# One-hot rows of the expert gates made by whole-tensor operations with two tokens interleaved, and an index look-up summed by halves

## The chip, the cores and the metric

The kernel runs on one core of one Trainium2 chip. The core has five engines that run side by side, each through its own list of instructions in order: TensorE (PE in the profile, with PEld for its weight loads), VectorE (DVE), ScalarE (ACT), GpSimd (POOL) and SyncE (SP, which here only starts transfers). They wait for each other through semaphores. The metric is the device time of one execution, in microseconds (us).

## The reference

The program is two transformer blocks on 256 tokens of width 1024. The change lies in the last stage of the second block, a mixture of 16384 tiny experts. Cut to what matters:

```python
PEER_HEADS, PEER_NKEYS, PEER_TOPK = 8, 128, 16        # experts = 128 x 128

q = (xb @ w_q).reshape(tb, PEER_HEADS, 2, PEER_DKEY // 2)
s = jnp.einsum('thpd,hpnd->thpn', q, sub_keys)
sv, si = lax.top_k(s, k)                               # 16 best row keys, 16 best column keys
cand = sv[:, :, 0, :, None] + sv[:, :, 1, None, :]
cand_idx = si[:, :, 0, :, None] * PEER_NKEYS + si[:, :, 1, None, :]
top_v, top_i = lax.top_k(cand, k)                      # 16 of the 256 pairs
experts = jnp.take_along_axis(cand_idx, top_i, axis=-1)
g = jax.nn.softmax(top_v, axis=-1)
a = gelu(einsum('td,thkd->thk', xb, u[experts]))
return einsum('thk,thkd->td', g * a, v[experts])
```

## The kernel before

**No gather.** The kernel computes the activations of all 16384 experts for all tokens and multiplies them with a matrix that is the gate where a token chose the expert and zero elsewhere. The stage has two long passes. `u_pass` (4 calls, 64 pairs of row keys j) makes `gelu(u h2)`: for each j, 8 blocks of 128x128 weights, and for each block three matmuls of 256 tokens (lines 171 to 173), since every fp32 weight is split into a high half `whi` (ACT, line 133) and a low half `wlo` (DVE, line 130). So one j is 24 matmuls, one `whi` and one `wlo`. `v_pass` (4 calls) multiplies the activations with the gates and then with `v` (line 1095). Both weights stream from HBM through `raw` (line 154, issued by SP), 1 MB for a pair of j.

**The gate matrix.** It is built beside `u_pass` by a generator that `feed` steps once or twice after each pair. First `topk_steps`, for 128 tokens at a time (`tt`): top 16 by DVE, softmax `e_`, and for each of the 128 choices of a token (8 heads x 16) the row and the column key. These are looked up by comparing a position with 0..15 (`eq`, lines 960 and 965: 16 planes of 128 choices, all but one plane zero) and by summing the 16 planes (`ix`, line 970). Gates and keys are then transposed by PE so that a partition is a choice and a column a token: `idxT` (row key), `jdxT` (column key), `gT` (the gate in two fp16 parts).

Then `g_steps`, 32 groups of TG = 8 tokens. For each token the gate matrix is a product of two one-hot matrices over its 128 choices. DVE makes the one-hot rows `o1` for a group with one whole-tensor compare (line 1001), four tokens interleaved: the fastest index of `o1` runs over 4 tokens. It makes the gated one-hot rows `og` with one small instruction for each token and each of the two gate parts (line 1005), 16 for a group, each a compare with a per-partition key and a product with a per-partition gate:

```python
nc.vector.tensor_scalar(og[:, t, c], iota16, jdxT[:, tc_:tc_ + 1], gT[:, c, tc_:tc_ + 1],
                        op0=OP.is_equal, op1=OP.mult)
```

PE multiplies them a step later, 16 matmuls of 128 columns for a group (line 1016), ACT copies the result to `gs` (line 1018) and ACT's queue stores it to the HBM tensor `gg_d` (line 1019, `ggd` in the trace). `v_pass` reads it back as `gh` (line 1075), 8 transfers of 2 MB, issued by SP.

**What sets the order.** A scheduler arranges each engine's instructions from a simulated timeline, with program order as its priority. `o1` and `og` have three buffers, `gs` two, `whi` and `wlo` three each, `raw` three. DVE runs its list in order, so a `wlo` that stands behind a group's one-hot work waits for it, and PE's third matmul of a block waits for that `wlo`.

Of the kernel before, what the change touches and what calls it, by code (L numbers as in the profile page):

```python
# [10 lines left out]
F32 = mybir.dt.float32  # L11
F32R = mybir.dt.float32r
BF16 = mybir.dt.bfloat16
F16 = mybir.dt.float16
I32 = mybir.dt.int32
U32 = mybir.dt.uint32
AF = mybir.ActivationFunctionType
# [3 lines left out]
P = 128  # L21
# [42 lines left out]
def block_kernel(ctx: ExitStack, tc: tile.TileContext, a: dict, out: bass.AP, dbg=None):  # L64
# [796 lines left out]
    ga_d = [dram.tile([P, QJ // 2, 2 * S], F32, name=f"gad{q}") for q in range(2)]  # L861
    gg_d = dram.tile([P, NG, NE * TG], F32, name="ggd")

    idxT = big.tile([P, S], F16, name="idxT")
    jdxT = big.tile([P, S], F32, name="jdxT")
    gT = big.tile([P, 2, S], F32, name="gT")
    iota16 = big.tile([P, P], F16, name="iota16")
    nc.vector.tensor_copy(iota16, iota)
    iota4 = big.tile([P, P, 4], F16, name="iota4")
    nc.vector.tensor_copy(iota4, iota[:, :, None].to_broadcast([P, P, 4]))  # L870
    st4 = ExitStack()
    tk = pool(st4, "tk")
    keys = tk.tile([P, 16, P], F32, name="keys")
# [33 lines left out]
    def topk_steps():  # L907
        for tt in range(2):
            tv = tk.tile([P, 8, 16], F32, tag="tv", bufs=2, name="tv")
            ti = tk.tile([P, 8, 16], U32, tag="ti", bufs=2, name="ti")  # L910
            si = tk.tile([P, 8, 2, 16], U32, tag="si", bufs=2, name="si")
            for h in range(8):
                sv = tk.tile([P, 2, 16], F32, tag="sv", bufs=2, name="sv")
                for p_ in range(2):
                    s2 = tk.tile([P, P], F32, tag="s2", bufs=2, name="s2")
                    top16(sv[:, p_], si[:, h, p_], scs[h][:, 2 * tt + p_], s2)
                yield
                cd = tk.tile([P, NROW, 8], F32, tag="cd", bufs=2, name="cd")
                cd2 = tk.tile([P, NROW * 8], F32, tag="cd2", bufs=2, name="cd2")
                cf = cd.rearrange("p r c -> p (r c)")  # L920
                nc.vector.tensor_scalar(cf[:, 0:16], sv[:, 1], sv[:, 0, 0:1], None, op0=OP.add)
                nc.vector.tensor_tensor(cd[:, 2:9], sv[:, 0, 1:8, None].to_broadcast([P, 7, 8]),
                                        sv[:, 1, None, 0:8].to_broadcast([P, 7, 8]), op=OP.add)
                nc.vector.tensor_scalar(cd[:, 9], sv[:, 0, 8:16], sv[:, 1, 0:1], None, op0=OP.add)
                top16(tv[:, h], ti[:, h], cf, cd2)
                yield

            e_ = tk.tile([P, 8, 16], F32, tag="te", name="te")
            nc.vector.tensor_tensor(e_, tv, tv[:, :, 0:1].to_broadcast([P, 8, 16]), op=OP.subtract)
            nc.scalar.activation(e_, e_, AF.Exp)  # L930

            rc = tk.tile([P, 2, 8, 16], U32, tag="rc", name="rc")
            nc.vector.tensor_scalar(rc[:, 0], ti, 3, None, op0=OP.logical_shift_right)
            nc.vector.tensor_scalar(rc[:, 1], ti, 7, None, op0=OP.bitwise_and)
            rf = tk.tile([P, 2, 8, 16], F32, tag="rf", name="rf")
            nc.vector.tensor_copy(rf, rc)
            sf_ = tk.tile([P, 8, 2, 16], F16, tag="sf", name="sf")
            nc.vector.tensor_copy(sf_, si)
            yield
            z = small.tile([P, 8], F32, tag="az", name="tz")  # L940
            nc.vector.reduce_sum(z, e_, axis=AX.X)
            rz = small.tile([P, 8], F32, tag="ar", name="trz")
            nc.vector.reciprocal(rz, z)
            nc.vector.tensor_scalar(rz, rz, GSCALE, None, op0=OP.mult)
            nc.vector.tensor_tensor(e_, e_, rz[:, :, None].to_broadcast([P, 8, 16]), op=OP.mult)

            ij = tk.tile([P, 2, P], F16, tag="ij", name="ij")
            r_, c_ = (rf[:, x].rearrange("p h k -> p (h k)") for x in range(2))
            t_ = tk.tile([P, 3, P], F32, tag="ijt", name="ijt")
            nc.vector.scalar_tensor_tensor(t_[:, 0], r_, 9.0, c_, op0=OP.is_equal, op1=OP.mult)  # L950
            nc.vector.tensor_scalar(t_[:, 1], r_, -1.0, 0.0, op0=OP.add, op1=OP.max)
            nc.vector.tensor_tensor(ij[:, 0], t_[:, 0], t_[:, 1], op=OP.add)
            nc.vector.tensor_tensor(t_[:, 1], c_, t_[:, 0], op=OP.subtract)
            nc.vector.tensor_scalar(t_[:, 2], r_, 1.0, 8.0, op0=OP.is_equal, op1=OP.mult)
            nc.vector.tensor_tensor(ij[:, 1], t_[:, 1], t_[:, 2], op=OP.add)
            yield
            back = [(e_, None)]
            for p_ in range(2):
                eq = tk.tile([P, 16, P], F16, tag="eq", name="eq")
                nc.vector.tensor_tensor(  # L960
                    eq.rearrange("p j (g f) -> p j g f", f=4), iota4[:, :16, None, :].to_broadcast([P, 16, P // 4, 4]),
                    ij[:, p_].rearrange("p (g f) -> p g f", f=4)[:, None].to_broadcast([P, 16, P // 4, 4]),
                    op=OP.is_equal)
                eh = eq.rearrange("p j (h k) -> p j h k", h=8)
                nc.vector.tensor_tensor(
                    eh, eh, sf_[:, :, p_].rearrange("p h j -> p j h")[:, :, :, None].to_broadcast([P, 16, 8, 16]),
                    op=OP.mult)
                yield
                ix = tk.tile([P, P], F32, tag="ix", bufs=2, name="ix")
                nc.vector.reduce_sum(ix, eq.rearrange("p j x -> p x j"), axis=AX.X)  # L970
                back.append((ix, p_))
                yield
            with tc.issue_after(last_mm[0].ins):
                for src, p_ in back:
                    pt = ps_d()
                    ts = slice(tt * P, (tt + 1) * P)
                    nc.tensor.transpose(pt[:, :P], src if p_ is not None else src.rearrange("p h k -> p (h k)"), ident)
                    if p_ is None:
                        gt16 = tk.tile([P, P], F16, tag="gt16", name="gt16")
                        nc.scalar.activation(gt16, pt[:, :P], AF.Copy)  # L980
                        nc.scalar.activation(gT[:, 0, ts], gt16, AF.Copy)
                        nc.vector.tensor_tensor(gT[:, 1, ts], pt[:, :P], gT[:, 0, ts], op=OP.subtract)
                    else:
                        nc.scalar.activation((idxT, jdxT)[p_][:, ts], pt[:, :P], AF.Copy)

    def g_steps():

        gp = pool(stg, "gp", 3)
        todo = None
        for i in range(NG + 1):  # L990
            new = None
            if i < NG:
                ts = slice(i * TG, (i + 1) * TG)

                def four(x):
                    return x.rearrange("p (g t) -> p g t", t=4)[:, :, None, :].to_broadcast([P, TG // 4, P, 4])

                io = iota4[:, None].to_broadcast([P, TG // 4, P, 4])
                o1 = gp.tile([P, TG // 4, P, 4], F16, tag="o1", name="o1")
                og = gp.tile([P, TG, 2, P], F16, tag="og", name="og")  # L1000
                nc.vector.tensor_tensor(o1, io, four(idxT[:, ts]), op=OP.is_equal)  # L1001
                for t in range(TG):
                    for c in range(2):
                        tc_ = i * TG + t
                        nc.vector.tensor_scalar(og[:, t, c], iota16, jdxT[:, tc_:tc_ + 1], gT[:, c, tc_:tc_ + 1],  # L1005
                                                op0=OP.is_equal, op1=OP.mult)
                new = i, o1, og
            if todo:
                i_, o1, og = todo
                gs = gp.tile([P, NE, TG], F32, tag="gs", bufs=2, name="gs")  # L1010
                with tc.issue_after(last_mm[0].ins):
                    for g4 in range(TG // 4):
                        ps = (ps_d, ps_b)[g4 % 2]()
                        for t4 in range(4):
                            for c in (1, 0):
                                nc.tensor.matmul(ps[:, t4 * P:(t4 + 1) * P], o1[:, g4, :, t4], og[:, g4 * 4 + t4, c],
                                                 start=(c == 1), stop=(c == 0))
                        nc.scalar.activation(gs[:, :, g4 * 4:g4 * 4 + 4], ps.rearrange("p (t j) -> p j t", t=4), AF.Copy)
                nc.scalar.dma_start(gg_d[:, i_], gs.rearrange("p j t -> p (j t)"))
            todo = new  # L1020
            yield
# [253 lines left out]
```

## Time and profile before

| | us |
|---|---|
| median of 3 runs (lowest to highest) | 1461.04 (1459.24 to 1467.02) |
| the profiled execution | 1463.96 |
| its span, first to last instruction | 1462.0 |
| PE / DVE / ACT busy | 1388.6 / 1076.4 / 705.0 |

The span is what the trace covers; about 2 us of the execution lie around it. Busy shares are averages over the whole program, so the reading goes stage by stage: the look-ups run from about 640 to 745 us, the 32 groups from 822 to 1000 us, the rest of `u_pass` ends near 1100 us, and `v_pass` fills what follows up to 1448 us. In the rows PE's matmul durations contain waiting in the pipeline; the distance from one start to the next is what a matmul costs PE. The same holds on DVE: the chain of waits gives the time that one instruction adds to the chain, which is shorter than its duration.

### The profile page before, as it was taken

The numbers are of one execution on the slowest core, as the hardware profiler recorded it, in microseconds if no ns is written. First come the engines' busy times: TensorE is split into PE (matmuls) and PEld (weight loads), VectorE is DVE, ScalarE is ACT, GpSimd is POOL, SyncE is SP. The second block draws the span as 40 slices with busy tenths as digits, with TensorE's granted clock in tenths as the row PEclk, the third lists the DMA queues.
The fourth block names the chain that finished last, engine by engine and source line by source line (L and its number), as shares of the span: only waits on it lengthen the run. The fifth ranks groups of instructions, "written<-read, shape, count | busy, mean of one in ns | idle before, by whom it ended". The sixth has DMA issues, their size and how long they took to land.

```text
span 1462.0 us, 24629 instructions
## 1 busy us (share of the span) xinstructions
PE 1388.6 (95%) x9776; PEld 1278.8 (87%) x9776; DVE 1076.4 (74%) x2154; ACT 705.0 (48%) x1032; POOL 23.7 (2%) x25
## 2 busy tenths in 40 slices
PE   7999999999999999999999888889799999999997
PEld 6967998999998889999999888889788888888886
DVE  6774779998977556899964799995835555566765
ACT  4444645454545555554544434444334455444443
POOL 1000000000000010000000000000000000000000
PEclk9999999999999999999999989999989999999999
DMA  7442447777886414344555456668986555588762
GB/s 244 160 168 87 151 167 281 266 264 277 297 288 216 160 49 173 130 160 168 180 187 187 166 202 241 243 245 273 350 300 229 185 203 187 196 277 295 266 247 86
DMA packets 88451, 308.88 MB, mean 211 GB/s; under 512 B 6416, under 2 KB 39824, under 8 KB 61200
## 3 DMA queue, kind: packets, MB, share of 16 engines
q1 hardware_dynamic: 78544, 279.26, 54.8%
q10 hardware_dynamic: 9792, 28.05, 5.1%
q8 instruction: 76, 1.25, 0.4%
q14 instruction: 39, 0.32, 0.1%
HBM read 281.08 MB, written 26.21 MB: 210 GB/s over the span
## 4 chain that ended last, share of the span: by engine, by line
PE 75%; DVE 17%; DMA 5%; issue 2%; ACT 0%; POOL 0%; SPq 0%; POOLq 0%; DVEq 0%; ACTq 0%
PE acc L1095 24%; PE psa L173 9%; PE psa L171 9%; PE psa L172 9%; DVE og L1005 7%; PE psc L173 5%; PE psc L171 5%; PE psc L172 5%; DVE wlo L130 4%; DMA gh<-ggd 2%; DMA raw<-in_uT 2%; PE psb L501 2%; DVE o L1001 1%; PE psd L771 1%; PE psb L759 1%
## 5 line engine op out<-in xcount | busy, mean ns | idle before, releaser
L133 ACT ACTIVATE whi<-raw 128x1024 fp32r<-128x1024 f32 (+1 forms) x426 | 447.8, 1053 | 541.3 <-PE psc L172 206.5
L130 DVE TENSOR_TENSOR wlo<-raw,whi 128x1024 fp32r<-128x1024 f32 (+1 forms) x426 | 518.6, 1226 | 224.9 <-ACT whi L133 221.6
L173 PE MATMUL psc<-h2h,wlo 128*128 128x256 f32 x1024 | 298.2, 292 | 33.1 <-DVE wlo L130 32.9
L171 PE MATMUL psc<-h2h,whi 128*128 128x256 f32 x1024 | 297.5, 291 | 7.0 <-ACT whi L133 6.6
L172 PE MATMUL psc<-h2l,whi 128*128 128x256 f32 x1024 | 295.9, 289 | 0.0
L173 PEld LDWEIGHTS psc<-h2h,wlo 128*128 128x128 f32 x1024 | 202.7, 198 | 37.7 <-DVE wlo L130 37.7
L171 PEld LDWEIGHTS psc<-h2h,whi 128*128 128x128 f32 x1024 | 203.0, 198 | 7.7 <-ACT whi L133 7.2
L172 PEld LDWEIGHTS psc<-h2l,whi 128*128 128x128 f32 x1024 | 203.2, 198 | 0.0
L1095 PE MATMUL acc<-wlo,wgh 128*128 128x512 f32 x512 | 160.3, 393 | 0.0
L1095 PE MATMUL acc<-whi,wgl 128*128 128x512 f32 x512 | 158.7, 390 | 0.0
L1095 PE MATMUL acc<-whi,wgh 128*128 128x512 f32 x512 | 138.5, 389 | 0.0
L1005 DVE TENSOR_SCALAR og<-iota,jdxT,gT 128x128 f16<-128x128 f16 x512 | 120.5, 391 | 0.0
L1095 PEld LDWEIGHTS acc<-whi,wgl 128*128 128x128 f32 x512 | 96.1, 188 | 20.2
L1095 PEld LDWEIGHTS acc<-whi,wgh 128*128 128x128 f32 x512 | 96.0, 188 | 20.1
L1095 PEld LDWEIGHTS acc<-wlo,wgh 128*128 128x128 f32 x512 | 94.5, 188 | 19.8
L171 PE MATMUL psa<-acth,whi 128*128 128x256 f32 x352 | 99.9, 284 | 2.0 <-DVE ft L638 1.2
L173 PE MATMUL psa<-acth,wlo 128*128 128x256 f32 x352 | 99.8, 284 | 0.8 <-DVE wlo L130 0.7
L172 PE MATMUL psa<-actl,whi 128*128 128x256 f32 x352 | 99.7, 283 | 0.0
L171 PE MATMUL psa<-xh,whi 128*128 128x256 f32 x240 | 71.1, 296 | 8.2 <-ACT whi L133 8.2
L173 PE MATMUL psa<-xh,wlo 128*128 128x256 f32 x240 | 70.4, 293 | 2.6 <-DVE wlo L130 2.6
L172 PE MATMUL psa<-xl,whi 128*128 128x256 f32 x240 | 71.0, 296 | 0.0
L171 PEld LDWEIGHTS psa<-acth,whi 128*128 128x128 f32 x352 | 67.5, 192 | 2.5 <-ACT whi L133 1.4
(416 smaller groups left out, 2479.4 us busy)
## 6 DMA issues: line engine op xcount, KB each, us to landing
raw<-in_uT SPq DMA_DIRECT2D x64, 1024.0 KB, 4.9
raw<-in_v SPq DMA_DIRECT2D x64, 1024.0 KB, 4.8
aw<-in_ada SPq DMA_DIRECT2D x48, 512.0 KB, 5.9
raw<-in_wgu SPq DMA_DIRECT2D x22, 1024.0 KB, 5.0
ggd<-gs ACTq DMA_DIRECT2D x32, 512.0 KB, 2.9
gh<-ggd SPq DMA_DIRECT2D x8, 2048.0 KB, 14.3
raw<-in_wA SPq DMA_DIRECT2D x14, 1024.0 KB, 5.1
raw<-in_wdn SPq DMA_DIRECT2D x11, 1024.0 KB, 7.1
```

The lines of the kernel that those rows point to most:

```text
L130: e.tensor_tensor(dst, src, hi.bitcast(F32), op=OP.subtract)
L133: nc.scalar.activation(dst_h, src, AF.Copy)
L171: nc.tensor.matmul(ps, wh, xs[0][:, k], start=(k == 0), stop=False)
L172: nc.tensor.matmul(ps, wh, xs[1][:, k], start=False, stop=False)
L173: last_mm[0] = nc.tensor.matmul(ps, wl, xs[0][:, k], start=False, stop=(k == K - 1))
L501: nc.tensor.matmul(s[:, i], q_[:, qb * P:(qb + 1) * P], k_[:, :n], start=(j == 0), stop=False)
L759: nc.tensor.matmul(s, q2[x_][hd, hp, qs_], kall[y_][hd, hp], start=(i == 0), stop=(i == 2))
L771: nc.tensor.matmul(o[:, h * 64:(h + 1) * 64], pts[:, kb * P:(kb + 1) * P], v2[:, kb, h * 64:(h + 1) * 64], start=(kb == 0), stop=(kb == 3))
L1001: nc.vector.tensor_tensor(o1, io, four(idxT[:, ts]), op=OP.is_equal)
L1005: nc.vector.tensor_scalar(og[:, t, c], iota16, jdxT[:, tc_:tc_ + 1], gT[:, c, tc_:tc_ + 1], op0=OP.is_equal, op1=OP.mult)
L1095: r = nc.tensor.matmul(acc[tt][n], x_, w_[:, n * 512:(n + 1) * 512], start=st, stop=sp)
```

## The change

`jdxT` and `idxT` become the two planes of one fp16 tensor, `gT` becomes fp16, and the constant of counting numbers is interleaved for two tokens (`iota2`) in place of four. For a group, DVE now makes `o1` and a second one-hot tensor `o2` by whole-tensor compares (lines 999 and 1000 of the new file) and `og` by two whole-tensor products of `o2` with the two gate parts (line 1002). All four are 128x1024 fp16. `o2` has two buffers. PE reads both operands with a step of two elements. The sum over the 16 planes of `eq` becomes three in-place additions of halves (8, 4 and 2 planes, line 968) and a last one into `ix` (line 969). An fp16 copy of the gates, `gt16`, is dropped.

```diff
+    idxT = big.tile([P, 2, S], F16, name="idxT")
+    gT = big.tile([P, 2, S], F16, name="gT")
+    iota2 = big.tile([P, P, 2], F16, name="iota2")
...
-                nc.vector.reduce_sum(ix, eq.rearrange("p j x -> p x j"), axis=AX.X)
+                for n in (8, 4, 2):
+                    nc.vector.tensor_tensor(eq[:, :n], eq[:, :n], eq[:, n:2 * n], op=OP.add)
+                nc.vector.tensor_tensor(ix, eq[:, 0], eq[:, 1], op=OP.add)
...
-                        gt16 = tk.tile([P, P], F16, tag="gt16", name="gt16")
-                        nc.scalar.activation(gt16, pt[:, :P], AF.Copy)
-                        nc.scalar.activation(gT[:, 0, ts], gt16, AF.Copy)
+                        nc.scalar.activation(gT[:, 0, ts], pt[:, :P], AF.Copy)
...
-                def four(x):
-                    return x.rearrange("p (g t) -> p g t", t=4)[:, :, None, :].to_broadcast([P, TG // 4, P, 4])
-                io = iota4[:, None].to_broadcast([P, TG // 4, P, 4])
-                nc.vector.tensor_tensor(o1, io, four(idxT[:, ts]), op=OP.is_equal)
-                for t in range(TG):
-                    for c in range(2):
-                        tc_ = i * TG + t
-                        nc.vector.tensor_scalar(og[:, t, c], iota16, jdxT[:, tc_:tc_ + 1], gT[:, c, tc_:tc_ + 1],
-                                                op0=OP.is_equal, op1=OP.mult)
+                def two(x):
+                    return x.rearrange("p (g t) -> p g t", t=2)[:, :, None, :].to_broadcast([P, TG // 2, P, 2])
+                io = iota2[:, None].to_broadcast([P, TG // 2, P, 2])
+                o2 = gp.tile([P, TG // 2, P, 2], F16, tag="o2", bufs=2, name="o2")
+                og = gp.tile([P, 2, TG // 2, P, 2], F16, tag="og", name="og")
+                nc.vector.tensor_tensor(o1, io, two(idxT[:, 0, ts]), op=OP.is_equal)
+                nc.vector.tensor_tensor(o2, io, two(idxT[:, 1, ts]), op=OP.is_equal)
+                for c in range(2):
+                    nc.vector.tensor_tensor(og[:, c], o2, two(gT[:, c, ts]), op=OP.mult)
...
-                                nc.tensor.matmul(ps[:, t4 * P:(t4 + 1) * P], o1[:, g4, :, t4], og[:, g4 * 4 + t4, c],
+                                nc.tensor.matmul(ps[:, t4 * P:(t4 + 1) * P], o1[:, 2 * g4 + t4 // 2, :, t4 % 2], og[:, c, 2 * g4 + t4 // 2, :, t4 % 2],
```

The scheduler sets the new work among the old. On DVE, in the middle of the groups, the list before has two groups between the `wlo` of one pair and of the next (names `o_9879` and so on are the buffers of `o1`):

```order
L130 TENSOR_TENSOR wlo<-raw,whi 128x1024 x2
L1001 TENSOR_TENSOR o_9879<-iota_6489,idxT 128x1024
L1005 TENSOR_SCALAR og<-iota_6487,jdxT,gT 128x128 x16
L1001 TENSOR_TENSOR o_9920<-iota_6489,idxT 128x1024
L1005 TENSOR_SCALAR og<-iota_6487,jdxT,gT 128x128 x16
L130 TENSOR_TENSOR wlo<-raw,whi 128x1024 x2
```

In the changed kernel the same stretch of DVE's list reads as follows (the first number of a group is `o1`, the second `o2`):

```order
L130 TENSOR_TENSOR wlo<-raw,whi 128x1024
L1000 TENSOR_TENSOR o_10149<-iota_6486,idxT 128x1024
L1000 TENSOR_TENSOR o_10240<-iota_6486,idxT 128x1024
L130 TENSOR_TENSOR wlo<-raw,whi 128x1024
L999 TENSOR_TENSOR o_10239<-iota_6486,idxT 128x1024
L1002 TENSOR_TENSOR og<-o_10149,gT 128x1024 x2
L999 TENSOR_TENSOR o_10330<-iota_6486,idxT 128x1024
L1002 TENSOR_TENSOR og<-o_10240,gT 128x1024 x2
L130 TENSOR_TENSOR wlo<-raw,whi 128x1024
```

Two groups stand between a pair's `wlo` and the next pair's as before, with 8 instructions where there were 34, and the two `wlo` of a pair are no longer neighbours. In the look-up for the second 128 tokens, DVE's list before has the sum over the 16 planes as one instruction:

```order
L960 TENSOR_TENSOR eq<-iota_6489,ij 128x2048
L955 TENSOR_TENSOR ij<-ijt 128x128
L130 TENSOR_TENSOR wlo<-raw,whi 128x1024
L965 TENSOR_TENSOR eq<-eq,sf 128x2048
L130 TENSOR_TENSOR wlo<-raw,whi 128x1024
L970 TENSOR_REDUCE ix<-eq 128x128
L130 TENSOR_TENSOR wlo<-raw,whi 128x1024
```

In the changed kernel the four additions stand there (lines 968 and 969), with other work between most of them:

```order
L962 TENSOR_TENSOR eq<-eq,sf 128x2048
L941 TENSOR_SCALAR trz<-trz 128x8
L130 TENSOR_TENSOR wlo<-raw,whi 128x1024
L968 TENSOR_TENSOR eq<-eq 128x1024
L942 TENSOR_TENSOR te<-te,trz 128x128
L130 TENSOR_TENSOR wlo<-raw,whi 128x1024
L968 TENSOR_TENSOR eq<-eq 128x512
L968 TENSOR_TENSOR eq<-eq 128x256
L130 TENSOR_TENSOR wlo<-raw,whi 128x1024
L969 TENSOR_TENSOR ix<-eq 128x128
```

No single instruction there is longer than a plane compare any more, and two of the additions are neighbours that depend on each other. On PE the number and the sizes of all matmuls stay; the first group stands behind the 1586th of the 3072 matmuls of `u_pass` (before: from the 1562nd to the 1588th, strewn), the last behind the 2400th (before: the 2402nd). SP's list keeps its order, with the first two `gh` behind the 55th `raw` of `u_pass`.

## Rows read from the trace of the kernel before

**Rows 1.** The page: span, then busy us (share) and instructions of each engine.

```profile
span 1462.0 us, 24629 instructions
PE 1388.6 (95%) x9776; PEld 1278.8 (87%) x9776; DVE 1076.4 (74%) x2154; ACT 705.0 (48%) x1032; POOL 23.7 (2%) x25
```

**Rows 2.** Busy time by stretch: look-ups (three), groups, rest of `u_pass`, `v_pass`.

```profile
core 0: us, PE busy (x) PEld busy (x) DVE busy (x) ACT busy (x) POOL busy (x), PEclk, DMA share, GB/s
595.00:822.00 227.00, 223.93 (x1866) 223.12 (x1865) 181.34 (x551) 110.54 (x135) 0.00 (x0) 1.00 0.49 172
660.00:700.00 40.00, 37.60 (x309) 36.99 (x308) 40.00 (x106) 16.69 (x20) 0.00 (x0) 1.00 0.44 153
700.00:740.00 40.00, 40.00 (x336) 40.00 (x335) 39.21 (x113) 21.82 (x28) 0.00 (x0) 1.00 0.56 197
826.10:1000.24 174.14, 146.84 (x1355) 140.67 (x1354) 170.90 (x566) 77.27 (x116) 0.00 (x0) 0.92 0.61 225
1000.24:1088.00 87.76, 75.89 (x572) 74.37 (x572) 49.08 (x58) 32.55 (x40) 0.00 (x0) 0.92 1.02 328
1104.00:1448.00 344.00, 344.00 (x1531) 284.12 (x1530) 213.78 (x219) 167.13 (x192) 0.00 (x0) 1.00 0.63 222
```

**Rows 3.** What PE waited for, 820 to 1005 us (total, times, longest).

```profile
PE psc L173 <- DVE wlo L130: 24.6, 12, 4.9
PE psd L1016 <- DVE og L1005: 1.0, 2, 0.8
PE psb L1016 <- DVE og L1005: 0.7, 4, 0.2
```

**Rows 4.** The chain of waits inside the groups: start, us added, engine, line.

```profile
822.42 0.60 DVE o L1001
823.02 3.58 DVE og L1005 x16
826.60 0.60 DVE o L1001
...
843.29 2.27 DVE wlo L130 x2
...
985.03 0.21 PE psc L173
...
995.12 0.12 PE psc L172
995.24 0.12 PE psc L173
...
999.31 0.48 PE psd L1016 x8
999.79 0.45 PE psb L1016 x8
```

**Rows 5.** Instructions on lines 171 and 1016, 826.1 to 1000.24 us (ns min/median/max).

```profile
L171 PE MATMUL psc<-h2h,whi x281: 277/283/416, 825.9 to 998.8; 128*128 128x256 f32 x141
L1016 PEld LDWEIGHTS <-o x512: 110/113/152, 826.1 to 1000.0; 128*128 128x128 f16 x171
L1016 PE MATMUL psd<-og,o x256: 216/219/314, 826.1 to 999.6; 128*128 128x128 f16 x128
L1016 PE MATMUL psb<-og,o x256: 216/219/314, 827.9 to 1000.0; 128*128 128x128 f16 x128
```

**Rows 6.** DVE's groups by line, same stretch: busy us, mean ns, idle before.

```profile
L1005 DVE TENSOR_SCALAR og<-iota,jdxT,gT 128x128 f16<-128x128 f16 x499 | 117.6, 393 | 0.0
L130 DVE TENSOR_TENSOR wlo<-raw,whi 128x1024 fp32r<-128x1024 f32 x36 | 44.8, 1312 | 1.7 <-ACT whi L133 1.7
L1001 DVE TENSOR_TENSOR o<-iota,idxT 128x1024 f16<-128x1024 f16 x31 | 23.8, 767 | 0.0
```

**Rows 7.** ACT's and DVE's groups by line, 595 to 822 us.

```profile
L133 ACT ACTIVATE whi<-raw 128x1024 fp32r<-128x1024 f32 x75 | 79.4, 1058 | 107.2 <-PE psc L172 88.7 <-PE psa L172 12.2 <-issue 3.4
...
L130 DVE TENSOR_TENSOR wlo<-raw,whi 128x1024 fp32r<-128x1024 f32 x75 | 91.2, 1221 | 43.0 <-ACT whi L133 42.8
L970 DVE TENSOR_REDUCE ix<-eq 128x128 f32<-128x2048 f16 x4 | 15.5, 3876 | 0.0
L965 DVE TENSOR_TENSOR eq<-eq,sf 128x2048 f16<-128x2048 f16 x4 | 9.2, 2292 | 0.0
L960 DVE TENSOR_TENSOR eq<-iota,ij 128x2048 f16<-128x2048 f16 x4 | 4.9, 1225 | 0.0
L929 DVE TENSOR_TENSOR te<-tv 128x128 f32<-128x128 f32 x2 | 0.5, 274 | 0.0
```

**Rows 8.** What PE waited for, 595 to 822 us.

```profile
PE psc L173 <- DVE wlo L130: 3.1, 4, 1.1
```

**Rows 9.** The chain of waits behind the groups: transfers in the rest of `u_pass`.

```profile
1005.82 14.51 DMA gh<-ggd
1025.28 15.88 DMA gh<-ggd
1049.52 28.41 DMA raw<-in_uT x2
```

More of the change, by code (lines that the diff above doesn't have):

```diff
@@ L862, in block_kernel @@
     gg_d = dram.tile([P, NG, NE * TG], F32, name="ggd")
[L864 to L870, printed above, removed]
+    idxT = big.tile([P, 2, S], F16, name="idxT")
+    gT = big.tile([P, 2, S], F16, name="gT")
+    iota2 = big.tile([P, P, 2], F16, name="iota2")
+    nc.vector.tensor_copy(iota2, iota[:, :, None].to_broadcast([P, P, 2]))
     st4 = ExitStack()
@@ L960, in topk_steps @@
                 nc.vector.tensor_tensor(
-                    eq.rearrange("p j (g f) -> p j g f", f=4), iota4[:, :16, None, :].to_broadcast([P, 16, P // 4, 4]),
-                    ij[:, p_].rearrange("p (g f) -> p g f", f=4)[:, None].to_broadcast([P, 16, P // 4, 4]),
+                    eq.rearrange("p j (g f) -> p j g f", f=2), iota2[:, :16, None, :].to_broadcast([P, 16, P // 2, 2]),
+                    ij[:, p_].rearrange("p (g f) -> p g f", f=2)[:, None].to_broadcast([P, 16, P // 2, 2]),
                     op=OP.is_equal)
@@ L978, in topk_steps @@
                     if p_ is None:
-                        gt16 = tk.tile([P, P], F16, tag="gt16", name="gt16")
-                        nc.scalar.activation(gt16, pt[:, :P], AF.Copy)
-                        nc.scalar.activation(gT[:, 0, ts], gt16, AF.Copy)
+                        nc.scalar.activation(gT[:, 0, ts], pt[:, :P], AF.Copy)
                         nc.vector.tensor_tensor(gT[:, 1, ts], pt[:, :P], gT[:, 0, ts], op=OP.subtract)
                     else:
-                        nc.scalar.activation((idxT, jdxT)[p_][:, ts], pt[:, :P], AF.Copy)
+                        nc.scalar.activation(idxT[:, p_, ts], pt[:, :P], AF.Copy)
     def g_steps():
@@ L993, in g_steps @@
                 ts = slice(i * TG, (i + 1) * TG)
-                def four(x):
-                    return x.rearrange("p (g t) -> p g t", t=4)[:, :, None, :].to_broadcast([P, TG // 4, P, 4])
-                io = iota4[:, None].to_broadcast([P, TG // 4, P, 4])
-                o1 = gp.tile([P, TG // 4, P, 4], F16, tag="o1", name="o1")
-                og = gp.tile([P, TG, 2, P], F16, tag="og", name="og")
-                nc.vector.tensor_tensor(o1, io, four(idxT[:, ts]), op=OP.is_equal)
-                for t in range(TG):
-                    for c in range(2):
-                        tc_ = i * TG + t
-                        nc.vector.tensor_scalar(og[:, t, c], iota16, jdxT[:, tc_:tc_ + 1], gT[:, c, tc_:tc_ + 1],
-                                                op0=OP.is_equal, op1=OP.mult)
+                def two(x):
+                    return x.rearrange("p (g t) -> p g t", t=2)[:, :, None, :].to_broadcast([P, TG // 2, P, 2])
+                io = iota2[:, None].to_broadcast([P, TG // 2, P, 2])
+                o1 = gp.tile([P, TG // 2, P, 2], F16, tag="o1", name="o1")
+                o2 = gp.tile([P, TG // 2, P, 2], F16, tag="o2", bufs=2, name="o2")
[4 more added lines that the diff above has]
+                    nc.vector.tensor_tensor(og[:, c], o2, two(gT[:, c, ts]), op=OP.mult)
                 new = i, o1, og
@@ L1012, in g_steps @@
                     for g4 in range(TG // 4):
-                        ps = (ps_d, ps_b)[g4 % 2]()
+                        ps = (ps_d, ps_b)[g4]()
                         for t4 in range(4):
                             for c in (1, 0):
-                                nc.tensor.matmul(ps[:, t4 * P:(t4 + 1) * P], o1[:, g4, :, t4], og[:, g4 * 4 + t4, c],
+                                nc.tensor.matmul(ps[:, t4 * P:(t4 + 1) * P], o1[:, 2 * g4 + t4 // 2, :, t4 % 2], og[:, c, 2 * g4 + t4 // 2, :, t4 % 2],
                                                  start=(c == 1), stop=(c == 0))
```

## The prediction

> **What bounds the kernel now.** I read the page first, then the stretches, then the waits in one stretch. The page says PE is busy 95% and DVE 74% of the span [rows 1]; averages over stages with different limits, so they decide nothing. The stretches do [rows 2]. In `v_pass` PE is busy all 344 of 344 us at full clock: nothing that DVE does beside it counts. In the look-ups PE is busy 223.93 of 227 us, and its waits for `wlo` sum to 3.1 us [rows 8]. In the groups, 826.10 to 1000.24 us, the picture turns: DVE is busy 170.90 of 174.14 us, PE 146.84, and PE's granted clock is 0.92. PE's waits there are 24.6 us for DVE's `wlo`, and next to nothing for `og` itself [rows 3]. A `wlo` has its data early (DVE idled 1.7 us for `whi` in the stretch [rows 6]) and stands in DVE's list behind one-hot work. So DVE bounds the groups, through `wlo`.
>
> What PE needs there: 281 matmuls of line 171, as many of 172 and 173, so 843, and 512 of line 1016 [rows 5]. At full clock one of the 843 starts 0.12 us after the other; behind a wait the distance is 0.21 us [rows 4], the lower of the two clock levels (1.2 against 2.4 GHz). The 16 of a group took 0.48 + 0.45 = 0.93 us, 0.058 us each. 843 x 0.12 = 101.2 us and 512 x 0.058 = 29.8 us: 131.0 us. The stretch took 174.1, so 43.1 us are waiting and lower clock, its consequence.
>
> What DVE needs: the chain shows what one instruction adds to it [rows 4]: 0.60 us for `o1`, 3.58 us for the 16 `og` (0.224 each), 1.13 us for a `wlo` (2.27 for two). A group is 4.18 us. 31 `o1` lie in the stretch [rows 6], and 843/24 = 35 `wlo`: 31 x 4.18 + 35 x 1.135 = 129.6 + 39.7 = 169.3 us, which is the measured 170.9 within 1%. The model holds.
>
> **The change part by part.**
>
> *The one-hot rows.* 17 instructions of a group go, four come. `o1` before is already a two-source fp16 instruction of 128x1024 with a broadcast key; the four new ones have its size and types. Taken at its price, a group costs 4 x 0.60 = 2.40 us, and DVE in the stretch 31 x 2.40 + 39.7 = 114.1 us, below PE's 131.0. PE becomes the bound. The row differs from the new instructions in one point: its broadcast runs over 4 neighbouring tokens, theirs over 2. What the trace bounds: line 960 does 2048 fp16 elements in 1225 ns with runs of 4 or more, line 965 the same number in 2292 ns with one element repeated 16 times [rows 7]. The difference, 1067 ns, is half of 2048 elements at the slower rate; for 1024 it is 0.53 us. So an instruction costs between 0.60 and 1.13 us. I take 0.60: all tensors are fp16 and have neighbouring elements in the fastest index, as in line 960 and unlike line 965. The other end is a rival. Two thresholds help: DVE stays under PE's 131.0 us as long as an instruction costs less than (131.0 - 39.7)/124 = 0.74 us, and the gain is gone at (169.3 - 39.7)/124 = 1.05 us. Nothing below 0.60 is in sight, since the row with the same size is the fastest of its kind; and below 0.74 it would change nothing.
>
> *The place of the work.* Two groups of 8 instructions stand between the `wlo` of pairs, at most 5 or 6 of them (3.6 us) ahead of one `wlo`. With three buffers a split may begin two tiles of 24 matmuls (2 x 2.88 us) and the groups between (up to 1.9 us) ahead of its use: 7.7 us for 1.06 (`whi` [rows 7]) + 3.6 + 1.13 = 5.8 us. It fits, by 2 us. A pair with two groups asks 5.76 + 1.86 = 7.6 us of PE and 4.8 + 2.3 = 7.1 us of DVE, so DVE stays almost full there; pairs with one group give slack. Waits of DVE on its own results are mostly covered, since another instruction stands between `o2` and its products. I leave 5 us of the 43 for waits that remain: in the look-ups, where DVE was full for 80 us (79.21 busy from 660 to 740 us [rows 2]), PE waited 3.1 us [rows 8].
>
> *PE.* The number, order and sizes of matmuls stay. The stationary operand was already read with a step (of four elements) and costs the 0.058 us of a group's matmul; the moving one had no step and now steps by two. Taken at nothing. The bounds: nothing, or twice the time, 512 x 0.058 = 29.8 us. I take nothing, by the row of the stepped stationary operand.
>
> *The look-up.* `ix` cost 3.88 us in four places [rows 7]. The four additions are 1024, 512, 256 and 128 elements: 0.60, 0.60 - 0.27 = 0.33, about 0.20, and at most 0.27 us (line 929, as many elements, fp32): 1.4 us, 1.9 at most if the neighbours wait for each other. Some 2 us less in four places, 8 us of DVE. Two of the four lie where DVE was full; of PE's 3.1 us of waiting [rows 8] I take 2 back. The compare in runs of two (line 957) is at its old price, or 1.07 us dearer each. The dropped fp16 copy of the gates (two ACT instructions) and the smaller constants are hidden, ACT being idle more than half of the stretch [rows 2].
>
> *Late next.* Behind the groups nothing changes: SP has the first two `gh` at the same place, and they wait for the last group's store, which stands at the same matmul. The stalls there (14.51, 15.88 and 28.41 us of transfers on the chain [rows 9]) move forward whole. In the groups the transfers become denser: 174.14 us at 225 GB/s are 39.2 MB; at the 328 GB/s that the next stretch reached [rows 2] they need 119 us, under PE's 131. They are the next bound, 9% away.
>
> *The sum*, against the profiled execution of 1463.96 us (span 1462.0): -43.1 + 5 - 2 = -40, so 1424 us. That execution was 2.9 us above the median of 1461.04.
>
> **Rivals.**
>
> *A. Runs of two are slow.* If DVE takes one element at a time, as in line 965, a group costs 4 x 1.13 = 4.53 us, DVE 31 x 4.53 + 39.7 = 180.1 us in the stretch where it needed 169.3, and the four compares of the look-up 4.3 us more, which the cheaper sum gives back. PE waits as now and 11 us longer: 1475 us. It decides from 1.05 us on. For it: no row shows a run of two. Against it: the condition that sets line 960 apart from 965 (neighbours in the fastest index) is met. The Trainium skill ("Vector Engine (DVE) Microarchitecture Reference", Performance modes) asks for 2-byte types, a step of one and more than one element in the innermost index, and says that two elements suffice for two sources; that would give 0.60.
>
> *B. Runs of two are read at a rate between.* Every run is now 4 bytes, read again and again, where it was 8. At 0.94 us, two thirds of the way between the ends, DVE needs 31 x 3.76 + 39.7 = 156 us and bounds the groups: -13 us, 1450. Against it: line 965 reads one 2-byte element 16 times over and its 1067 ns above line 960 are exactly the slower rate, with nothing added for reading a place again. The same page (Measured stream behaviour on trn2) speaks for it: a port streams at full rate only if neighbours come in runs of at least two 4-byte words, and took 1.73 against 1.054 ns a column where single words hop. By that, as an estimate, the 0.53 us of 1024 elements would become 0.87 and the instruction 0.94; no run here shows whether re-reading a word counts as a hop.
>
> *C. PE reads the stepped rows at half rate:* +29.8 us for PE, 131.0 + 29.8 = 160.8 us, 13 below the 174.1, with 3 of waits that remain: 1454 us. The stepped stationary operand speaks against it.
>
> *D. PE still waits.* Transfers of 39 MB crowd into 131 us, or DVE's full pairs hold `wlo`, and half of what I expect is lost: 1442 us. For it: the 9% and the 2 us of slack above.
>
> **How the numbers follow.** Forecast 1424 us (its own range 1412 to 1434): 0.65. D 0.15, B 0.07, C 0.04, A 0.09. A measurement of this kernel tells 0.5%, 7 us, from no change. Faster by more (below 1454): forecast, D, B and half of C, 0.89; within: 0.03; slower: A, 0.08. The range for 8 in 10 reaches from 1412 (no waits remain, and of the rest of `u_pass`, where PE is busy only 75.89 of 87.76 us [rows 2], some come in sooner) to 1448, which takes in D.
>
> **What would show it.** `o1`, `o2` and `og` at about 0.76 us a row (0.60 on the chain); the groups shrunk from 174 to about 136 us with PE over 95% busy and a clock near 1.0; PE's waits for `wlo` there under 6 us; `gh` starting some 40 us earlier, the rest of `u_pass` at 88 us. Wrong it would be if these rows read above 0.9 us with DVE still full (A, B), if the group's 16 matmuls take over 1.2 us with DVE idle (C), or if ACT's `whi` waits for `raw` (D).

## The result and the profile after

| | before | after |
|---|---|---|
| median (lowest to highest), us | 1463.62 (1459.24 to 1467.02), 5 runs | 1413.68 (1412.18 to 1420.62), 5 runs |
| profiled execution, us | 1463.96 | 1420.62 |

The ratio of the runs is 0.9664, with a 95% interval of 0.9638 to 0.969: 3.4% faster. The forecast was 1424 us in a range of 1412 to 1448.

The page of the changed kernel begins with the span and with the busy time of each engine:

```profile
span 1418.8 us, 24208 instructions
PE 1375.2 (97%) x9776; PEld 1270.8 (90%) x9776; DVE 1013.1 (71%) x1749; ACT 704.9 (50%) x1030; POOL 23.8 (2%) x25
```

PE runs the same 9776 matmuls; DVE runs 405 instructions fewer [rows 1]. The stretches say where it counts: look-ups, groups, rest of `u_pass`, `v_pass`, with the columns of [rows 2]:

```profile
595.00:822.00 227.00, 227.00 (x1890) 227.00 (x1889) 174.00 (x567) 111.03 (x136) 0.00 (x0) 0.99 0.50 172
825.00:956.90 131.90, 131.90 (x1357) 130.88 (x1356) 117.07 (x159) 77.75 (x116) 0.00 (x0) 1.00 0.82 297
956.90:1056.60 99.70, 89.10 (x673) 87.87 (x672) 53.96 (x62) 38.09 (x46) 0.00 (x0) 0.91 0.97 315
1056.60:1409.00 352.40, 352.40 (x1570) 291.06 (x1568) 218.45 (x227) 170.74 (x198) 0.00 (x0) 1.00 0.63 220
```

In the groups PE is busy all the time, at full clock, and DVE has 15 us to spare. In the answer on PE's waits between 820 and 956.9 us there is not one row; before there were 24.6 us for `wlo` [rows 3]. It is DVE that waits now, for ACT's `whi` and for PE to free a buffer of `o1` (820 to 965 us; total, times, longest):

```profile
DVE wlo L130 <- ACT whi L133: 14.8, 13, 3.5
DVE o L999 <- PE psb L1012: 5.8, 8, 1.6
```

DVE's groups by line, 825 to 956.9 us, beside [rows 6]; all three kinds of the new instruction take 0.68 to 0.69 us a row, less than the 0.76 that the forecast looked for:

```profile
L130 DVE TENSOR_TENSOR wlo<-raw,whi 128x1024 fp32r<-128x1024 f32 x36 | 43.9, 1220 | 7.3 <-ACT whi L133 7.2
L1002 DVE TENSOR_TENSOR og<-o,gT 128x1024 f16<-128x1024 f16 x64 | 40.7, 684 | 0.0
L999 DVE TENSOR_TENSOR o<-iota,idxT 128x1024 f16<-128x1024 f16 x29 | 20.0, 688 | 6.0 <-PE psb L1012 5.8
L1000 DVE TENSOR_TENSOR o<-iota,idxT 128x1024 f16<-128x1024 f16 x30 | 19.9, 684 | 0.0
```

From one start to the next each costs 0.60 us, the price that the forecast used: in these three lines of DVE's timeline one `o1` takes 0.61 us and two `og` take 1.20 us until the next instruction starts.

```profile
861.39 0.69 DVE L999 TENSOR_TENSOR o<-iota,idxT 128x1024 f16<-128x1024 f16 x1
862.00 1.29 DVE L1002 TENSOR_TENSOR og<-o,gT 128x1024 f16<-128x1024 f16 x2
863.20 0.69 DVE L999 TENSOR_TENSOR o<-iota,idxT 128x1024 f16<-128x1024 f16 x1
```

In the look-ups (595 to 822 us) the additions of halves take 1.4 us in each of the four places, without the last one into `ix` (0.28 us), and the compare in runs of two keeps its old price [rows 7]; the answer on PE's waits there is empty:

```profile
L968 DVE TENSOR_TENSOR eq<-eq 128x1024 f16<-128x1024 f16 (+2 forms) x12 | 5.5, 460 | 0.1
L957 DVE TENSOR_TENSOR eq<-iota,ij 128x2048 f16<-128x2048 f16 x4 | 4.9, 1217 | 0.0
```

**Where the time went.** To compare kernels I cut each trace at four starts of PE's instructions: the first key matmul (line 898 before), the last transpose of a key (line 977), the last matmul of the last group (line 1016), the first matmul of `v_pass` (line 1095). The starts are read per line; these are the ones of after:

```profile
L895 PE MATMUL psd<-keys,pq x64: 270/275/275, 598.2 to 641.4; 128*128 128x128 f32 x64
L976 PE MATMUL psd<-cst,ix x4: 272/272/273, 712.4 to 820.7; 128*128 128x128 f32 x4
L1012 PE MATMUL psb<-og,o x256: 217/218/220, 828.9 to 956.7; 128*128 128x128 f16 x128
L1091 PE MATMUL acc<-whi,wgh x512: 388/389/397, 1056.6 to 1408.5; 128*128 128x512 f32 x171
```

| us, profiled execution | up to the keys | look-ups | groups | rest of `u_pass` | `v_pass` to the end | from the keys to the end |
|---|---|---|---|---|---|---|
| before | 594.8 | 226.5 | 178.7 | 99.8 | 362.2 | 867.2 |
| after | 598.2 | 222.5 | 136.0 | 99.9 | 362.2 | 820.6 |
| after, once more | 597.7 | 222.5 | 135.9 | 100.1 | 362.2 | 820.7 |
| groups only | 589.1 | 226.6 | 136.0 | 104.3 | 362.3 | 829.2 |
| sum only | 600.1 | 222.5 | 180.2 | 97.6 | 362.2 | 862.5 |
| four tokens | 591.0 | 222.5 | 165.7 | 99.7 | 362.2 | 850.1 |
| one token | 594.9 | 222.5 | 220.4 | 20.1 | 369.8 | 832.8 |
| one compare more | 593.8 | 223.3 | 155.6 | 77.8 | 360.7 | 817.4 |
| two compares more | 595.6 | 223.3 | 188.5 | 32.1 | 377.1 | 821.0 |
| before, slow feed | 588.3 | 226.6 | 192.4 | 56.2 | 370.6 | 845.8 |
| after, slow feed | 589.1 | 222.6 | 158.9 | 71.9 | 362.8 | 816.2 |
| late products | 591.2 | 222.5 | 136.0 | 86.6 | 361.9 | 807.0 |
| late products, slow feed | 594.2 | 222.6 | 158.9 | 63.8 | 361.9 | 807.2 |

From before to after: 4.0 us in the look-ups, 42.7 in the groups, nothing behind them: 46.6. The first column belongs to stages that no kernel here edits, and differs by up to 12 us from one profiled execution to another (588.3 to 600.1); that is why a single profiled execution says less of the total than of its stages. The groups' 42.7 us stand against the 43.1 that the forecast counted there as waiting and lower clock.

### The profile page after: what moved, and what is told of

It is laid out like the page before. It is cut to its first block, busy times and chain, and to the rows that moved or that the text cites. A ratio compares the mean times of both kernels' runs of the same rounds, so it can differ in the third digit from the quotient of the medians.

```text
span 1418.8 us, 24208 instructions
## 1 busy us (share of the span) xinstructions
PE 1375.2 (97%) x9776; PEld 1270.8 (90%) x9776; DVE 1013.1 (71%) x1749; ACT 704.9 (50%) x1030; POOL 23.8 (2%) x25
## 4 chain that ended last, share of the span: by engine, by line
PE 88%; DVE 5%; DMA 4%; issue 1%; ACT 1%; POOL 0%; SPq 0%; ACTq 0%; POOLq 0%; DVEq 0%
PE acc L1091 24%; PE psa L173 9%; PE psa L171 9%; PE psa L172 9%; PE psc L173 8%; PE psc L171 8%; PE psc L172 8%; DMA aw<-in_ada 2%; PE psb L501 2%; DVE wlo L130 2%; PE psd L1012 1%; PE psb L1012 1%; DMA gh<-ggd 1%; PE psd L771 1%; PE psb L759 1%
## 5 line engine op out<-in xcount | busy, mean ns | idle before, releaser
L130 DVE TENSOR_TENSOR wlo<-raw,whi 128x1024 fp32r<-128x1024 f32 (+1 forms) x426 | 517.4, 1217 | 240.6 <-ACT whi L133 236.9
L171 PE MATMUL psc<-h2h,whi 128*128 128x256 f32 x1024 | 294.3, 288 | 6.4 <-ACT whi L133 6.4
L173 PE MATMUL psc<-h2h,wlo 128*128 128x256 f32 x1024 | 293.8, 288 | 4.2 <-DVE wlo L130 4.2
L172 PE MATMUL psc<-h2l,whi 128*128 128x256 f32 x1024 | 292.7, 286 | 0.0
L171 PEld LDWEIGHTS psc<-h2h,whi 128*128 128x128 f32 x1024 | 199.8, 195 | 7.0 <-ACT whi L133 7.0
L173 PEld LDWEIGHTS psc<-h2h,wlo 128*128 128x128 f32 x1024 | 199.5, 195 | 4.9 <-DVE wlo L130 4.9
L172 PEld LDWEIGHTS psc<-h2l,whi 128*128 128x128 f32 x1024 | 199.8, 195 | 0.0
L1091 PEld LDWEIGHTS acc<-whi,wgh 128*128 128x128 f32 x512 | 96.0, 188 | 20.1
L171 PE MATMUL psa<-acth,whi 128*128 128x256 f32 x352 | 99.9, 284 | 2.0 <-DVE ft L638 1.2
L173 PE MATMUL psa<-acth,wlo 128*128 128x256 f32 x352 | 99.9, 284 | 1.9 <-DVE wlo L130 1.9
L172 PE MATMUL psa<-actl,whi 128*128 128x256 f32 x352 | 99.8, 284 | 0.2 <-DVE actl L293 0.2
L316 DVE SCALAR_TENSOR_TENSOR jk<-aw,row_c 128x1024 bf16<-128x1024 f32 x48 | 58.6, 1220 | 14.8 <-DMA aw<-in_ada 14.4
```

Source lines behind the costliest of these rows:

```text
L130: e.tensor_tensor(dst, src, hi.bitcast(F32), op=OP.subtract)
L171: nc.tensor.matmul(ps, wh, xs[0][:, k], start=(k == 0), stop=False)
L172: nc.tensor.matmul(ps, wh, xs[1][:, k], start=False, stop=False)
L173: last_mm[0] = nc.tensor.matmul(ps, wl, xs[0][:, k], start=False, stop=(k == K - 1))
L316: nc.vector.scalar_tensor_tensor(jk, aw, 1.0, c_, op0=OP.mult, op1=OP.mult, accum_out=dst[:, t:t + 1])
L1091: r = nc.tensor.matmul(acc[tt][n], x_, w_[:, n * 512:(n + 1) * 512], start=st, stop=sp)
```

## The experiments

**The change once more.** An unedited copy, to see what of the result repeats.

> The changed kernel once more, unedited, for a second trace. Theory: the change is worth what the stages show, 42.7 us in the groups (817.1 to 1000.2 us before, 816.5 to 956.9 after) and 4.1 us in the look-ups, 46.8 us in all; the first trace after began its look-ups 3.45 us later because of transfers of in_ada in a stage that the change does not touch. So this trace should again show groups of 140.4 us and no waits of PE in them, whatever the start. Rival: part of the difference of 50 us between the medians is a real gain elsewhere; then the rest of u_pass (99.7 us before) or the time up to the look-ups would be shorter than before here.

Measured: 1417.76 us, ratio 0.9693 (0.9666 to 0.972). The four stages repeat to 0.2 us (table); again no wait of PE in the groups. So the change is worth 46.6 us by stages, and the 50 us between the medians contain some 3 us that no stage shows.

**The two halves of the change.** First the groups as changed with the old sum, then the kernel before with the new sum alone:

```diff
-                for n in (8, 4, 2):
-                    nc.vector.tensor_tensor(eq[:, :n], eq[:, :n], eq[:, n:2 * n], op=OP.add)
-                nc.vector.tensor_tensor(ix, eq[:, 0], eq[:, 1], op=OP.add)
+                nc.vector.reduce_sum(ix, eq.rearrange("p j x -> p x j"), axis=AX.X)
```

> The changed groups with the old single sum over 16 planes. Theory: the groups alone carry 42.7 us; the look-ups fall back to about 222 us with 3 us of PE waiting for wlo, so 3 to 4 us slower than the changed kernel, about 1417 us. Rival (the sum is where the gain is, since it stood on the chain of waits): 10 us or more slower than the changed kernel.

> The kernel before with only the sum by halves. Theory: 3 to 4 us faster than before (ratio 0.997 to 0.998), PE's waits in the look-ups gone, groups still about 183 us from the second transpose on. Rival: nothing (PE waited for the rest of DVE's list, not for the sum), ratio 1.000.

Measured: groups only 1419.68 us, ratio 0.9712 (0.9688 to 0.9736); sum only 1458.25 us, ratio 0.997 (0.9954 to 0.9987). The table gives the sum its 4.0 us in the look-ups, both ways round, and the groups their 42.7 without it. The rest of `u_pass` took 104.3 us with groups only and 97.6 with sum only; in SP's list of both, one `gh` stands one `raw` earlier, and I followed that no further. With the sum alone PE's wait for `wlo` in the groups stays as it was [rows 3]:

```profile
PE psc L173 <- DVE wlo L130: 26.6, 12, 4.9
```

**Four tokens in place of two.** Everything whole-tensor as in the change, but with the old interleaving:

```diff
-                o2 = gp.tile([P, TG // 2, P, 2], F16, tag="o2", bufs=2, name="o2")
-                og = gp.tile([P, 2, TG // 2, P, 2], F16, tag="og", name="og")
+                o2 = gp.tile([P, TG // 4, P, 4], F16, tag="o2", bufs=2, name="o2")
+                og = gp.tile([P, 2, TG // 4, P, 4], F16, tag="og", name="og")
...
```

> The changed kernel with four tokens interleaved instead of two, all else whole-tensor as in the change. Theory: the number of DVE instructions matters and the run of 2 against 4 does not: each instruction 0.68 us long as with two, same time as the changed kernel within 0.3%. Rival (runs of two cost something on DVE, or PE's step of two elements against four does): instructions shorter than 0.68 us, or the 16 matmuls of a group away from 0.93 us, and a time that moves with them.

Measured: 1445.3 us, ratio 0.9885 (0.9844 to 0.9925). My theory fell, and the rival on PE stands. The 8 matmuls of half a group cost the chain 0.94 to 0.96 us here:

```profile
880.58 0.95 PE psb L1012 x8
881.52 0.94 PE psd L1012 x8
```

and half of that in the changed kernel:

```profile
868.06 0.47 PE psd L1012 x8
868.54 0.46 PE psb L1012 x8
```

512 matmuls at 0.118 instead of 0.058 us are 30 us more, and the groups are 29.7 us longer with PE never waiting (162.10 us busy of 162.10 at full clock):

```profile
817.50:979.60 162.10, 162.10 (x1361) 160.25 (x1360) 120.00 (x161) 83.32 (x118) 0.00 (x0) 1.00 0.67 245
```

DVE's instructions did not change (684 ns for `og`, as with two). In the kernel before, the stationary operand had the step of four elements and the moving one none, at 0.058 us a matmul [rows 4]; so it is the moving operand, whose 128 columns come at half rate with a step of 8 bytes and at full rate with a step of 4. (The stationary operand has the step of four in both kernels of this comparison; no run steps the moving one alone.)

**One token.** No interleaving: the key or the gate of a token is repeated 128 times in place.

```diff
-                    return x.rearrange("p (g t) -> p g t", t=2)[:, :, None, :].to_broadcast([P, TG // 2, P, 2])
+                    return x[:, :, None].to_broadcast([P, TG, P])
...
```

> The changed kernel without interleaving: the key of one token is repeated 128 times in place, so its tensor has no neighbours in the fastest index, as in the product of the look-up (line 962). Theory: DVE takes one element at a time, about 1.2 us an instruction, 1.13 on the chain: 31 x 4.53 + 39.7 = 180 us of DVE in the groups, which were 169 before and 114 after; DVE bounds the groups again, PE waits for wlo, and the time is 10 us above the kernel before less 4 of the sum, about 1469 us. Rival (the count of instructions is what mattered, 4 against 17): near the changed kernel, 1415 to 1425 us.

Measured: 1429.55 us, ratio 0.9739 (0.9709 to 0.977). The price of an instruction is the one expected, 1217 ns (822 to 1000 us):

```profile
L1004 DVE TENSOR_TENSOR og<-o,gT 128x1024 f16<-128x1024 f16 x52 | 61.2, 1217 | 0.0
```

The time is not. With 4.53 us of DVE a group, more than the 4.18 before, this kernel is 2.6% faster than the kernel before. The reason stands in PE's list: the groups lie behind the 1612th to the 3072nd matmul of `u_pass`, where they lay from the 1562nd to the 2402nd. Only the shape of DVE's operands was edited, so the scheduler seems to have priced these instructions higher and to have spread the groups for it; its prices themselves are not on record. The last matmul of a group starts at 1037.8 us:

```profile
L1014 PE MATMUL psb<-og,o x256: 219/219/219, 829.0 to 1037.8; 128*128 128x128 f16 x128
```

and PE's waits between 820 and 1000 us are none, although DVE has no idle moment (822 to 1000 us: PE busy 177.89 of 178 us, DVE 178.00):

```profile
822.00:1000.00 178.00, 177.89 (x1672) 174.61 (x1671) 178.00 (x157) 95.22 (x131) 0.00 (x0) 1.00 0.77 262
```

A full DVE alone does not make PE wait. Look-ups to end, 832.8 us: 12 more than after, 7.6 of them in `v_pass`, where PE waits once for 18.1 us because the first gates come late.

**More work for DVE.** One or two more compares for each group, into a tile that nobody reads.

```diff
+                for _ in range(1):        # 2 in the second kernel
+                    oj = gp.tile([P, TG // 2, P, 2], F16, tag="oj", bufs=2, name="oj")
+                    nc.vector.tensor_tensor(oj, io, two(idxT[:, 1, ts]), op=OP.is_equal)
```

> The changed kernel with one more whole-tensor compare for each group into a tile that nobody reads. Theory: DVE needs 31 x 3.00 + 39.7 = 132.7 us in the groups where PE needs 131: at the edge, 1 to 6 us slower than the changed kernel. Rival (DVE was the bound of the changed groups already): 31 x 0.60 = 19 us slower.

> Two such compares more for each group. Theory: DVE needs 31 x 3.60 + 39.7 = 151.3 us against PE's 131: 20 us slower than the changed kernel, PE's waits for wlo back. Rival (DVE's load does not set the time, its order does): no more than with one extra compare.

Measured: 1410.42 us, ratio 0.9615 (0.9594 to 0.9636), and 1416.55 us, ratio 0.9651 (0.9617 to 0.9686). Neither costs what I expected, and from the keys to the end the kernel with one compare more is even 3.2 us shorter than the change (817.4 against 820.6); why, I did not follow. The last group stands at the 2560th and at the 2834th matmul. The stage table shows the exchange: with two compares `u_pass` behind the look-ups is 15 us shorter than after (220.6 against 235.9), while the last three of the six `gh` that were in it start in `v_pass`, and `v_pass` is 14.9 us longer. These runs do not test the threshold of 0.74 us, since the place of the groups moved with the load.

**The pace alone.** So is it the place, not the load? The kernel before with one number changed, and the changed kernel likewise (1.4):

```diff
-            feed(1.2 if q * QJ + j < 60 else 1.7)
+            feed(1.2 if q * QJ + j < 60 else 1.3)
```

> The kernel before with one number changed: 1.3 instead of 1.7 steps of the generator after a pair of the later half, so that the 32 groups lie over 1126 matmuls (1562nd to 2688th) instead of 840. Theory (the groups lost time because DVE got more work for a pair than PE's pair takes, not because of its total): DVE needs 31 x 4.18 + 47 x 1.135 = 183 us there, PE 1126 x 0.12 + 29.8 = 165 us, so 18 us are lost where 43 were: 25 us faster than before, about 1439 us, if the later gh costs nothing. Rival (DVE's total work counts, as my prediction put it with a stretch of fixed length): nothing, 1463 us.

> The changed kernel with 1.4 instead of 1.7 steps, groups from the 1586th to the 2592nd matmul. Theory (PE is the bound of the changed groups and DVE has room): nothing to win in the groups; the groups and the rest of u_pass together stay at 236 us or lose the 3 us that the kernel with one extra compare lost, since fewer transfers meet; 1410 to 1415 us. Rival (the extra compare hid something else): over 1416 us.

Measured: 1437.9 us, ratio 0.9845 (0.9795 to 0.9895), and 1411.64 us, ratio 0.9663 (0.9622 to 0.9704). The kernel before, with all of its 16 small instructions for a group, wins about half of the change's gain by pace alone (21.4 of 46.6 us by stages, with 8.4 us lost in `v_pass`). PE's wait for `wlo` from 815 to 1110 us, in the kernel before and in this one:

```profile
PE psc L173 <- DVE wlo L130: 29.9, 16, 4.9
PE psc L173 <- DVE wlo L130: 18.0, 11, 3.6
```

That the second is the 18 of the expectation is chance, since those 18 us were all the time lost in the groups, waiting and lower clock together. Counted in that way the groups, whose matmuls start from 819.7 to 1007.3 us and need 1126 x 0.12 + 29.8 = 164.9 us of PE, lose 187.6 - 164.9 = 23 us, where they lost 43:

```profile
L1016 PE MATMUL psd<-og,o x256: 219/219/248, 819.7 to 1006.8; 128*128 128x128 f16 x128
L1016 PE MATMUL psb<-og,o x256: 219/219/247, 821.4 to 1007.3; 128*128 128x128 f16 x128
```

In the first 180 us of the groups DVE is still full, with PE behind it:

```profile
820.00:1000.00 180.00, 164.17 (x1559) 160.68 (x1559) 180.00 (x573) 87.56 (x127) 0.00 (x0) 0.98 0.68 249
```

So the 43 us were lost because DVE was given more work for a pair of `u_pass` (9.4 us at 1.7 groups) than PE's pair takes (7.3 us); at 1.3 groups it is 7.7 against 7.0 us, and some loss stays. The total of DVE's work, the same in both, was not the matter. For the changed kernel the slow feed is not told apart from the change by this interval. By stages it is 4.4 us shorter (816.2 against 820.6), where the expectation had nothing to win; the gain lies in the groups and the rest of `u_pass` together (230.8 against 235.9), and its cause stays open.

**The products of `v_pass`, later.** In the changed kernel the rest of `u_pass` needs 672 x 0.12 = 80.6 us and takes 99.9. The waits of PE and of DVE there, 956.9 to 1056 us:

```profile
PE psc L171 <- ACT whi L133: 6.4, 3, 2.2
PE psc L173 <- DVE wlo L130: 4.2, 3, 2.3
```

```profile
DVE ga L1078 <- DMA gh<-ggd: 5.9, 2, 3.1
```

DVE's list has 32 products of activations and gates (`ga`, the first two quarters) between the last `wlo` of `u_pass`; they wait for `gh`, and the next `wlo` waits behind them. The edit puts each product behind the split of two pairs earlier (`los` collects these splits), and was also run with the feed of 1.4:

```diff
-            nc.vector.tensor_tensor(gv, gv, gh[...].rearrange("p g j t -> p j g t"), op=OP.mult)
+            with tc.issue_after(los[-2].ins):
+                nc.vector.tensor_tensor(gv, gv, gh[...].rearrange("p g j t -> p j g t"), op=OP.mult)
```

> The changed kernel with the products of activations and gates (line 1078) put into DVE's list one by one, each behind the split of two pairs of v_pass earlier, instead of all 32 of the first two quarters before v_pass begins. SP's list then has two gh of 2 MB in u_pass, the others in v_pass. Theory: the rest of u_pass behind the groups takes 100 us for 672 matmuls that need 80.6, because DVE waits for gh in front of a wlo and four gh crowd out raw; with two gh it takes 85 to 92 us: 8 to 15 us faster than the changed kernel, about 1404 us. Rival (the gates' transfers cost the same wherever they are): what u_pass wins, v_pass loses; no change.

> Both edits of the two kernels before this one: late products and 1.4 steps. Theory: the effects are on different waits and add, 0 to 5 us under the kernel with late products alone. Rival: the groups end later, so gh has less time before v_pass and the wait for it moves to the first products of v_pass; slower than late products alone.

Measured: 1402.06 us, ratio 0.9601 (0.9559 to 0.9644), and 1402.6 us, ratio 0.9602 (0.9559 to 0.9646). The rest of `u_pass` falls from 99.9 to 86.6 us, and `v_pass` does not pay for it (361.9 against 362.2). What is left of PE's waits between 956.9 and 1056 us:

```profile
PE psc L172 <- ACT whi L134: 3.1, 1, 3.1
PE psc L174 <- DVE wlo L131: 0.8, 1, 0.8
```

By stages this version is 13.6 us under the change; by medians, beside other runs of before, 12 to 16. The slow feed adds nothing to it (807.2 against 807.0 us): the theory's 0 to 5 us at their lower end, and no sign of the rival. Two causes were moved together: DVE's order and the place of four `gh`, 8 MB, which went from `u_pass` into `v_pass`. Which carried more stays open. The trace has signs of both. On the chain of waits of the changed kernel a `gh` transfer, the products behind it and a `wlo` follow each other:

```profile
993.91 14.60 DMA gh<-ggd
1008.54 2.82 DVE ga L1078 x5
...
1013.36 1.23 DVE wlo L130
```

And the DMA engines, busy 0.97 of the rest of `u_pass` in the changed kernel, are less busy with late products (0.80, from the last group to `v_pass`):

```profile
949.70:1036.30 86.60, 82.73 (x677) 82.32 (x675) 37.57 (x34) 37.63 (x46) 0.00 (x0) 0.98 0.80 272
```

## Why the prediction was right, and where it was not

**What bounded the kernel: right.** DVE bounded the groups through `wlo`: PE's waits for it vanished with the load, shrank from 29.9 to 18.0 us (815 to 1110 us) when the old load was paced, and stayed (26.6 us) when only the sum was changed.

**The sum of the groups: right in its main term.** 43.1 us were to be had and 42.7 came. The reserve of 5 us for waits that remain was wrong; none remained. I had taken it from the look-ups, where DVE was full, although my own count left DVE 17 us of room in the groups; the trace shows 15. The look-up gave 4.0 us where I took 2. All of the 3.1 us of PE's waits for `wlo` went, and 0.9 us more. The clock does not explain these 0.9 us: from the first key matmul to the last transpose the granted clock was 1.00 before as after. PE's starts do. At the longest of the four waits before, they are 1.38 us apart in place of 0.12, of which the list of waits has 1.10, and the next step is 0.23:

```profile
696.63 0.28 PE L172 MATMUL psc<-h2l,whi 128*128 128x256 f32 x1
698.01 0.39 PE L173 MATMUL psc<-h2h,wlo 128*128 128x256 f32 x1 [1.10 <-DVE wlo L130]
698.24 0.28 PE L171 MATMUL psc<-h2h,whi 128*128 128x256 f32 x1
```

Over the four waits (1.37, 0.49, 1.38 and 0.95 us from start to start) that makes about 4 us. These two terms, the reserve and the look-up, are 7 of the 10 us between the forecast and the median. The other 3 are those that the medians (49.9 us) show beyond the stages (46.6); no median execution was traced, and what they are stays open. The median stands only 1.7 us above the lower end of the range, which was set for no waits and a sooner rest of `u_pass`; the first came, the second did not.

**Runs of two (rivals A and B): the price was right for A, its consequence wrong.** 0.68 us with runs of two and with runs of four, 1.22 us without. B is dead: reading one 4-byte word again and again costs no more than reading two words. The figures of the Trainium skill that I set against the change ("Vector Engine (DVE) Microarchitecture Reference", Measured stream behaviour on trn2) are for streams that hop to other words; a word that is read again cost nothing more here, 684 ns with either run. Rival A was to end at 1475 us, slower than before. The run with one token has A's price and ends at 1429.55, faster than before. The step that failed is the assumption that the 843 matmuls of the stretch stay the same whatever an instruction costs: the groups were set elsewhere when DVE's instructions changed. It held for the change, where the last group stands at the 2400th matmul, and for no experiment that made DVE's instructions dearer or more.

**PE's stepped reads (rival C): right conclusion, wrong row.** I took the stepped stationary operand of the kernel before as evidence for the moving one. The run with four tokens shows that the moving operand behaves otherwise: at a step of four elements it costs 30 us, which is the upper bound of that term (29.8) to the microsecond; at a step of two it is free. Had the change kept four tokens, this term would have taken 29.7 of the 42.7 us. The Trainium skill ("SBUF — State Buffer", The DMA port swizzle) has a note by which one can step up to 8 bf16 elements for free; for the moving operand of these matmuls the measurement with fp16 disagrees: 0.118 us at a step of 4 elements against 0.058 us at 2.

**Late next: right.** The rest of `u_pass` moved forward whole (99.8 and 99.9 us). Transfers, 9% away by my count, did not get in the way: 297 GB/s in the groups with no wait for `raw`. What was late next behind the groups was DVE's products with the `gh` that they wait for, as the late products show; the runs do not tell DVE's order from the transfers.

**Rival D** did not come about: no wait of PE in the groups.

## What to carry to other kernels

Count an engine's work against the work that it accompanies, pair by pair, not in total: here the same instructions, fed more slowly, lost 23 us in the groups in place of 43. Where a scheduler places the work, a dearer instruction is not only slower but elsewhere, so look at the new order before pricing a rival by the old place. When a layout is interleaved to please one engine, check what step it gives the engine that reads it: the two-token form is full rate on DVE and PE, the four-token form only on DVE.

## What the runs showed of the hardware beyond expectation

The step of the moving operand: 128 columns of fp16 at a step of 8 bytes take PE twice as long (0.118 us) as at 4 bytes or none (0.058 us), while a step of 8 bytes on the stationary operand did not slow the matmuls of the kernel before (0.058 us), its weight loads taking 113 ns a row there [rows 5] and 97 ns with a step of 4 bytes:

```profile
L1012 PEld LDWEIGHTS <-o x512: 96/97/101, 828.4 to 956.6; 128*128 128x128 f16 x171
```
